# A decoder layer on one core: the sums of weight quarters in DRAM moved from the feed-forward part to the cross attention

## The chip, the cores and the metric

The kernel runs on one core of a Trainium2 chip. The core has five engines, each with its own queue that is worked through in order: TensorE (PE in the profile; loading of its stationary operand is shown apart as PEld), VectorE (DVE), ScalarE (ACT), GpSimd (POOL) and SyncE (SP). Transfers are issued from the queues of SP, ACT and POOL, and all of them run on the same 16 DMA engines of the core. An engine reaches an instruction only when those before it on its own queue are done, and waits there until the data that it names is ready.

The metric is the device time of one execution in microseconds; the median of the runs is compared.

## The reference

One decoder layer with 256 tokens and 256 memory tokens, D = 1024, all in float32:

```
z = x @ w_in                                     # pooling channels, q, k, v
mix = concat(pool(z_u), attention(z_q, z_k, z_v)) @ w_out
h1 = norm(alpha * x  + mix)
h2 = norm(alpha * h1 + cross_attention(h1, mem) @ w_xo)     # 4 heads of 256
h3 = norm(alpha * h2 + (silu(h2 @ w_gate) * (h2 @ w_up)) @ w_down)   # inner width 2816
```

The cross attention takes its queries from h1 @ w_xq, its keys and values from mem @ w_xkv.

## The kernel before

**Weights as two parts.** A product in float32 is made of three products of a faster type: each weight tile is rounded to a high part on ACT (line 171, `w49h`), and the remainder is a low part from DVE (line 173, `w49l`). The class `Stream` does this for all weights in one fixed order. A weight tile has a number: w43 to w50 are the query weights of the cross attention (two tiles for each of four heads), w51 to w58 its output projection, w59 to w102 gate and up, w103 to w123 six of the eleven chunks of the down projection in summed form, and so on.

**How the stream runs.** `fetch` issues the load of a tile on SP (line 103) into one of 7 raw buffers; a raw buffer comes free when its tile has been split. `prepare` gives a tile its high and low parts in one of 8 pairs of buffers, and then calls `fetch_ahead`. While a projection uses tile n, the tile 8 further on is cast. Where such a cast is called in the program, there it stands in the order of ACT and DVE, between their other work. `ws.before(n, load)` attaches another load to tile n: it is issued on SP just ahead of tile n's own load. The norm's gain and bias come in this way (ahead of w47 and w51 for the second norm).

**Stages.** Input projection and self attention; the mixing projection and first norm; the values of the memory tokens (`xv`) with the transposes of h1; then the queries of four heads (`do_xq`, `pxq`), with scores (`xscores`, `xs`), softmax, transposes and the products with the values between them; the output projection `xo`, during which the second norm's sums are made; the gate and up projections (`pg`) in eleven chunks; the down projection and third norm. The query of a head is drained from PSUM by ACT (line 849) and DVE (lines 850 and 852) before its scores can start (line 862). A norm needs one power of -0.5 of a column, which POOL computes (line 752).

**The sums in DRAM.** Seven of the eleven chunks of the down projection use a scheme with seven products in place of eight (Strassen's in Winograd's form). It needs sums of quarters of the weight. For six chunks these sums are made in DRAM, by DMAs that add to their target: `sum_z` and `sum_w` are DRAM buffers of 3 MB. Two plain copies, issued on SP, put two quarters in each, and four accumulating DMAs issued on POOL complete them. With the quarters numbered 0 to 3, sum_z becomes (1+2, 2+3), and sum_w becomes (0+1+2+3, 1+2+3). The sums are read as weight tiles from w105 on.

In the kernel before, the copy into sum_z is issued ahead of w62, the one into sum_w ahead of w63, and the four accumulations stand at the third chunk of gate and up (`add_quarters`). An accumulation waits for the copy or accumulation whose data it reads or adds to.

Of the kernel before, what the change touches and what calls it, by code (L numbers as in the profile page):

```python
# [11 lines left out]
OP = mybir.AluOpType  # L12
# [38 lines left out]
class Stream:  # L51
# [130 lines left out]
    def get(self, numbers, k):  # L182

        n = self.src[numbers[0]].shape[1]
        self.prepare(numbers[k // n] + 1)
        self.asked += 1
        if not self.held and self.asked % self.pace == 0:
            self.prepare(min(self.used + self.ahead, len(self.tiles) + 1))
        return self.parts_of(numbers, k)
# [18 lines left out]
def decoder_layer(  # L208
# [3 lines left out]
    nc = tc.nc  # L212
# [14 lines left out]
    def bank(name):  # L227
        return pb.tile([P, 512], F32, tag="b", name=name)

    def accbank(name):  # L230
        return pa.tile([P, 512], F32, tag="acc", name=name)


    ws = Stream(nc, rp, wp)

    def cols(w, c):

        return ws.add(w[c])

    def rows(w, k0, c0, nk=1, width=D):  # L240
        return ws.add(w[k0 * P:(k0 + nk) * P, c0:c0 + width].rearrange("(k p) n -> p k n", p=P), 1)
# [22 lines left out]
    c_xq = [cols(w_xq, c) for c in range(4)]  # L264
    c_xo = [rows(w_xo, k, 0) for k in range(KD)]
    c_gu = [ws.add(w_gu[c], 4) for c in range(NFC)]
    dram = ctx.enter_context(tc.tile_pool(name="dram", bufs=1, space=bass.MemoryType.DRAM))
    sum_z, sum_w = [dram.tile([P, 2, len(SUMMED), 512], F32, name=f"sum_{name}") for name in "zw"]
# [17 lines left out]
    class Both:  # L286
# [9 lines left out]
        def pair(self, k, ts=ALL):  # L296
            t, j = self.tiles[k // 4], k % 4
            return t[:, j, 0, ts], t[:, j, 1, ts]
# [51 lines left out]
    ws.before(c_dn[LAST[0]][1], load_norm("b", 3, ln3_b))  # L350


    ws.before(c_gu[0][3], lambda: nc.sync.dma_start(sum_z, w_sum[:, 1:3]))
    ws.before(c_gu[1][0], lambda: nc.sync.dma_start(sum_w, w_sum[:, 0:2]))

    def add_quarters():
        def add(dst, src):
            nc.gpsimd.dma_start(dst, src, accum_op=OP.add, max_dma_last_dim=8192)

        add(sum_z, w_sum[:, 2:4])  # L360
        for i in range(2):
            add(sum_w[:, i], sum_z[:, 1])
        add(sum_w[:, 0], w_sum[:, 1])

    ident = cp.tile([P, P], F32, name="ident")
    make_identity(nc, ident)
# [19 lines left out]
    def three(ps, w, y, start, stop, part=False):  # L386

        (wa, wb), (ya, yb) = w, y
        nc.tensor.matmul(ps, wa, ya, start=start, stop=False, skip_group_check=part)  # L389
        nc.tensor.matmul(ps, wa, yb, start=False, stop=False, skip_group_check=part)  # L390
        nc.tensor.matmul(ps, wb, ya, start=False, stop=stop, skip_group_check=part)  # L391
# [4 lines left out]
    def proj_both(pss, numbers, yT, group=KD):  # L396

        for k0 in range(0, KD, group):  # L400
            for k in range(k0, k0 + group):
                hi, _ = ws.get(numbers, k)
                for b, ps in enumerate(pss):
                    nc.tensor.matmul(ps, hi[:, b * P:(b + 1) * P], yT.both(k), start=k == 0, stop=False,  # L404
                                     skip_group_check=True)
                yield
            for k in range(k0, k0 + group):
                _, lo = ws.parts_of(numbers, k)
                for b, ps in enumerate(pss):
                    nc.tensor.matmul(ps[:, S:], lo[:, b * P:(b + 1) * P], yT.pair(k)[0], start=False,  # L410
                                     stop=k == KD - 1, skip_group_check=True)
                ws.done(numbers, k)
                if ws.pace == 1:
                    ws.next()
                yield

    def proj_n(pss, numbers, yT, last=True):

        for k in range(KD):
            for t, ps in pss.items():  # L420
                three(ps, yT.pair(k, slice(t * P, (t + 1) * P)), ws.get(numbers, k), k == 0, k == KD - 1)
            if last:
                ws.done(numbers, k)
            yield

    def proj_rows(acc, chunks, get, pieces, first, last, free, again=False):

        last_k = sum(ws.rows(numbers) for numbers in chunks) - 1
        k0 = 0
        for numbers in chunks:  # L430
            nk = ws.rows(numbers)
            for t in sorted({piece[0] for piece in pieces}):
                for j in range(nk):
                    k = k0 + j
                    y = pair(get(k), ALL, slice(t * P, (t + 1) * P))
                    hi, lo = ws.get(numbers, j)
                    for piece in pieces:
                        if piece[0] == t:
                            s = slice(*piece[1:])
                            three(acc[piece], y, (hi[:, s], lo[:, s]), first and k == 0, last and k == last_k,  # L440
                                  again)
                    if free and t == pieces[-1][0]:
                        ws.done(numbers, j)
                    yield
            k0 += nk

    def run(gen, n=None):

        while n is None or n > 0:
            if next(gen, gen) is gen:  # L450
                return False
            n = None if n is None else n - 1
        return True

    def split(h, l, ps):
        nc.scalar.copy(h, ps)  # L456
        nc.vector.tensor_sub(l, ps, r32(h))  # L457
# [267 lines left out]
    class Norm:  # L725
# [13 lines left out]
        def sum(self, c0, c1, acc):  # L739
            s = slice(c0, c1)  # L740
            nc.vector.scalar_tensor_tensor(self.r[:, s], self.tok[:, s], ALPHA, acc, op0=OP.mult, op1=OP.add)
# [39 lines left out]
    def project(chunks, get, held, pieces=PIECES):  # L781

        acc = {piece: accbank("acc") for piece in PIECES}
        if pieces != PIECES:
            (*_, (_, _, c), _), last = pieces, PIECES[-1]
            acc[pieces[-2]], acc[pieces[-1]] = acc[last][:, :c - last[1]], bank("acc")[:, :last[2] - c]
        head, rest = chunks[:-held], chunks[-held:]
        done = sum(ws.rows(numbers) for numbers in head)  # L790
        if head:
            yield from proj_rows(acc, head, get, PIECES, True, pieces != PIECES, True)
        ws.prepare(ws.used + ws.ahead)
        ws.prepare(ws.used + ws.ahead, nc.gpsimd)
        ws.held = True
        for piece in pieces:
            yield from proj_rows(acc, rest, lambda k: get(done + k), [piece], not head or piece[1] % 512 != 0, True,
                                 piece == pieces[-1], bool(head) and pieces != PIECES)
            yield piece, acc[last] if pieces != PIECES and piece == pieces[-2] else acc[piece]
# [77 lines left out]
    def xattend(h):  # L877
        po = bank("xo").rearrange("p (d t) -> p d t", d=2)
        for dd in range(2):
            for s in range(2):  # L880
                c = h * 256 + dd * P
                three(po[:, dd, :], pair(xv, ALL, s, slice(c, c + P)), pair(xpt[h], ALL, s), s == 0, s == 1)
        split(oT[0][:, 2 * h:2 * h + 2, :], oT[1][:, 2 * h:2 * h + 2, :], po)
# [18 lines left out]
    h2T = Both("h2T")  # L902
    h2 = ap.tile([P, T, D], F32, tag="a8", name="h2")
    xo = project(c_xo, lambda k: (oT[0][:, k], oT[1][:, k]), 4)
    xattend(1)
    run(xo, 1)
    xprobs_t(2)
# [56 lines left out]
    def gated_row(t, ps):  # L964

        sg = sg0[:, t, :]
        nc.scalar.activation(sg, ps[:, :CW], AF.Silu, bias=0.0, scale=1.0)
        nc.vector.tensor_mul(sg, sg, ps[:, CW:])
# [51 lines left out]
    ws.held = False  # L1020
    run(proj_n({1: first[1]}, c_gu[0], h2T))
    gated_row(1, first[1])
    left = None
    for c in range(1, NFC):
        pss = [(accbank if c % 2 else bank)("pg") for _ in range(4)]
        if c == 3:
            ws.widen(late)
            add_quarters()
        gu = proj_both(pss, c_gu[c], h2T, KD if c < NFC - 3 else 2)
        run(gu, 2)  # L1030
        if left:
            left.multiply()
        run(gu, 2)
        if left:
            left.split()
        else:
            run(gu, 4)
            gated_t()
        if c == NFC - 1:
            run(gu, 7)  # L1040
            ws.held = True
        run(gu)
        left = Gated(c, pss)
        left.add()
# [200 lines left out]
```

## Time and profile before

| | |
|---|---|
| median of 3 runs | 378.22 us (378.13 to 378.23) |
| the profiled execution | 378.57 us, its span 376.8 us |
| TensorE busy | 368.5 us, 98% of the span |
| DVE, ACT, POOL busy | 79%, 55%, 6% |
| granted TensorE clock, mean | 0.999 |
| moved by DMA | 90.80 MB, of it 7.86 MB by POOL's queue |

The profile is one execution. Its span runs from the first to the last instruction of the core, so it is a little shorter than the time of the execution. Its views are: busy time of each engine; the span in 40 equal slices of 9.4 us, with the busy share of each engine and of the DMA engines in tenths; the chain of work that ended last, followed back through what released each step; groups of instructions; what each engine waited for; timelines of single engines; and the DMA issues, with the time from issue to landing. In a row such as `w52h<-w52r 128x1024` the names are tiles of the program, `h`, `l` and `r` being the high part, the low part and the raw tile, and `SPq` is SP's queue issuing a DMA. In rows with two numbers in front, these are start and duration in us; what stands in square brackets is the idle time of the engine ahead of the row and what ended it.

### The profile page before, as it was taken

How to read it: one execution, taken by the hardware profiler on the slowest of the kernel's cores; microseconds unless marked ns; L12 is line 12 of the kernel's file. 1: busy time of each engine (PE TensorE's matmuls, PEld its weight loads, DVE VectorE, ACT ScalarE, POOL GpSimd, SP SyncE). 2: the span in 40 equal slices, each digit the busy share in tenths (PEclk: the TensorE clock that was granted, in tenths of full speed). 3: DMA queues.
4: the chain of work that ended last, by engine and by line, in shares of the span. 5: the costliest groups of instructions: out<-in, count | busy, mean ns of one | idle time of the engine just before them, and what ended most of it. 6: DMA issues, size and time to landing. Idle time of an engine off the chain costs nothing.

```text
span 376.8 us, 5614 instructions
## 1 busy us (share of the span) xinstructions
PE 368.5 (98%) x2058; PEld 317.2 (84%) x2058; DVE 298.2 (79%) x481; ACT 206.6 (55%) x330; POOL 24.5 (6%) x31
## 2 busy tenths in 40 slices
PE   9999999999999999999999999989999999999994
PEld 8997878787888889988888888868888888888882
DVE  6768799965699677865887468688888889989994
ACT  5746677644164636644145446465567668865510
POOL 1000033400010000000120101010000000000021
PEclk9999999999999999999999999999999999999999
DMA  7997674668509965998149999999655668996302
GB/s 268 414 416 270 217 286 139 198 221 285 165 0 301 374 214 181 348 334 315 57 79 232 340 272 355 291 318 335 236 192 172 199 195 255 300 401 260 94 0 111
DMA packets 26715, 90.80 MB, mean 241 GB/s; under 512 B 2624, under 2 KB 3392, under 8 KB 25920
## 3 DMA queue, kind: packets, MB, share of 16 engines
q1 hardware_dynamic: 25040, 82.13, 61.8%
q0 software_dynamic: 1216, 7.86, 10.3%
q10 hardware_dynamic: 432, 0.46, 0.3%
q8 instruction: 16, 0.26, 0.3%
q14 instruction: 11, 0.09, 0.1%
HBM read 89.39 MB, written 15.20 MB: 278 GB/s over the span
## 4 chain that ended last, share of the span: by engine, by line
PE 96%; DVE 1%; DMA 1%; ACT 1%; issue 0%; POOLq 0%; ACTq 0%
PE pg L404 20%; PE pg L410 10%; PE pqk L510 6%; PE m L389 5%; PE m L391 5%; PE m L390 5%; PE acc L389 4%; PE acc L390 4%; PE acc L391 4%; PE pxk L404 4%; PE pxq L404 4%; PE pxq L410 2%; PE pu L404 2%; PE pxk L410 2%; PE xv L389 2%; PE xv L391 2%
## 5 line engine op out<-in xcount | busy, mean ns | idle before, releaser
L456 ACT CAST g<-sg 128x512 fp32r<-128x512 f32 x16 | 9.9, 620 | 20.7 <-DVE sg L1010 14.8
L752 POOL TENSOR_TENSOR rs<-rs,mhalf 128x1 f32<-128x1 f32 x6 | 5.0, 832 | 238.5 <-DVE rs L751 238.5
L457 DVE TENSOR_TENSOR g<-sg,g 128x512 fp32r<-128x512 f32 x16 | 11.1, 692 | 9.6 <-ACT g L456 9.6
L991 DVE TENSOR_TENSOR sg<-pg,sg 128x256 f32<-128x256 f32 x40 | 14.1, 416 | 0.0
L990 ACT COPY sg<-pg 128x256 f32<-128x256 f32 x40 | 11.8, 378 | 0.6 <-PE pg L410 0.6
L995 ACT ACTIVATE sg<-sg 128x512 f32<-128x512 f32 x10 | 6.4, 635 | 10.0 <-DVE sg L991 10.0
L547 ACT ACTIVATE xpr<-xs,mx 128x256 f32<-128x256 f32 x8 | 3.7, 469 | 14.3 <-DVE mx L558 14.3
L547 ACT ACTIVATE pr<-pr,mx 128x128 f32<-128x128 f32 (+1 forms) x16 | 7.1, 445 | 7.6 <-DVE mx L578 7.6
L456 ACT CAST h2T<-tp 128x512 fp32r<-128x512 f32 x4 | 2.3, 586 | 13.0 <-PE tp L467 12.9
L757 DVE SCALAR_TENSOR_TENSOR r<-r,mv,gb 128x512 f32<-128x512 f32 (+2 forms) x12 | 8.2, 722 | 0.0
L744 DVE BATCH_NORM_STATS2 st<-r 128x6 f32<-128x512 f32 (+1 forms) x12 | 8.0, 670 | 0.3
L623 POOL TENSOR_TENSOR win<-upad 128x542 f32<-128x542 f32 x2 | 4.0, 1998 | 57.0 <-DVE upad L654 57.0
L996 DVE TENSOR_TENSOR sg<-sg 128x512 f32<-128x512 f32 x10 | 6.9, 691 | 0.8
L552 DVE RECIPROCAL sm<-sm 128x2 f32<-128x2 f32 x12 | 2.0, 166 | 6.0 <-ACT xpr L547 4.5
L862 PE MATMUL xs<-xkTh,xq 128*128 128x256 f32 x32 | 6.4, 282 | 0.0
L456 ACT CAST h1T<-tp 128x512 fp32r<-128x512 f32 x4 | 2.4, 588 | 7.1 <-PE tp L467 7.1
L762 DVE SCALAR_TENSOR_TENSOR h<-r,rs,gb 128x512 f32<-128x512 f32 x8 | 5.7, 747 | 0.1
L623 POOL TENSOR_TENSOR win<-win 128x269 f32<-128x269 f32 (+3 forms) x4 | 5.8, 1445 | 0.2
L662 ACT CAST xkTh<-pxk 128x256 fp32r<-128x256 f32 x8 | 2.6, 377 | 5.5 <-PE pxk L410 5.5
L664 DVE TENSOR_TENSOR xkl<-pxk,xkTh 128x256 f32<-128x256 f32 x8 | 3.0, 416 | 3.1 <-ACT xkTh L662 3.1
L862 PEld LDWEIGHTS xs<-xkTh,xq 128*128 128x128 f32 x32 | 5.2, 190 | 0.2
L171 ACT CAST w39h<-w39r 128x1024 fp32r<-128x1024 f32 x1 | 1.0, 1049 | 7.8 <-PE acc L391 7.8
(1132 smaller groups left out, 1286.4 us busy)
## 6 DMA issues: line engine op xcount, KB each, us to landing
sum_z<-in_w_sum SPq DMA_DIRECT2D x1, 3072.0 KB, 13.5
sum_w<-in_w_sum SPq DMA_DIRECT2D x1, 3072.0 KB, 18.8
sum_z<-in_w_sum POOLq DMA_DIRECT2D x1, 3072.0 KB, 21.1
sum_w<-sum_z POOLq DMA_DIRECT2D x2, 1536.0 KB, 15.6
gb<-in_ln_g SPq DMA_DIRECT2D x3, 512.0 KB, 6.2
gb<-in_ln_b SPq DMA_DIRECT2D x3, 512.0 KB, 9.2
sum_w<-in_w_sum POOLq DMA_DIRECT2D x1, 1536.0 KB, 14.6
wr<-in_w_qkv SPq DMA_DIRECT2D x5, 256.0 KB, 4.4
```

What stands on the lines that cost most here:

```text
L389: nc.tensor.matmul(ps, wa, ya, start=start, stop=False, skip_group_check=part)
L390: nc.tensor.matmul(ps, wa, yb, start=False, stop=False, skip_group_check=part)
L391: nc.tensor.matmul(ps, wb, ya, start=False, stop=stop, skip_group_check=part)
L404: nc.tensor.matmul(ps, hi[:, b * P:(b + 1) * P], yT.both(k), start=k == 0, stop=False, skip_group_check=True)
L410: nc.tensor.matmul(ps[:, S:], lo[:, b * P:(b + 1) * P], yT.pair(k)[0], start=False, stop=k == KD - 1, skip_group_check=True)
L456: nc.scalar.copy(h, ps)
L457: nc.vector.tensor_sub(l, ps, r32(h))
L510: nc.tensor.matmul(qk[i][:, f, :], w[:, c * P:(c + 1) * P], y, start=k == 0 and f == 0 and w is hi and y is x_hi, stop=k == KD - 1 and w i ...
L547: nc.scalar.activation(dst[:, j, :], src[:, j, :], AF.Exp, bias=mx[:, j:j + 1], scale=sign, accum_out=sm[:, j:j + 1])
L862: nc.tensor.matmul(ps[:, t, :], q[:, kk, t * P:(t + 1) * P], k[:, 2 * h + kk], start=n == 0, stop=q is q_lo and kk == 1, skip_group_check= ...
L990: nc.scalar.copy(y[:, f, :], ps[:, S:])
L991: nc.vector.tensor_add(y[:, f, :], ps[:, :S], y[:, f, :])
```

## The change

The same two copies and four accumulations are made, of the same bytes. Only their places differ:

- the copy into sum_z is issued ahead of w49 (the fourth head's query weights) instead of w62, and the copy into sum_w ahead of w52 (the second tile of the output projection) instead of w63;
- the accumulation into sum_z and the one into the second half of sum_w stand in front of the cross attention of the second head, where the output projection is set up, and so ahead of the second norm on POOL's queue;
- the two accumulations into the first half of sum_w stand behind the first gate chunk, and so behind the second norm on POOL's queue.

```diff
-    ws.before(c_gu[0][3], lambda: nc.sync.dma_start(sum_z, w_sum[:, 1:3]))
-    ws.before(c_gu[1][0], lambda: nc.sync.dma_start(sum_w, w_sum[:, 0:2]))
-
-    def add_quarters():
-        def add(dst, src):
-            nc.gpsimd.dma_start(dst, src, accum_op=OP.add, max_dma_last_dim=8192)
-
-        add(sum_z, w_sum[:, 2:4])
-        for i in range(2):
-            add(sum_w[:, i], sum_z[:, 1])
-        add(sum_w[:, 0], w_sum[:, 1])
+    ws.before(c_xq[3][0], lambda: nc.sync.dma_start(sum_z, w_sum[:, 1:3]))
+    ws.before(c_xo[1][0], lambda: nc.sync.dma_start(sum_w, w_sum[:, 0:2]))
+
+    def accumulate(dst, src):
+        nc.gpsimd.dma_start(dst, src, accum_op=OP.add, max_dma_last_dim=8192)
...
     xo = project(c_xo, lambda k: (oT[0][:, k], oT[1][:, k]), 4)
+    accumulate(sum_z, w_sum[:, 2:4])
+    accumulate(sum_w[:, 1], sum_z[:, 1])
     xattend(1)
...
     run(proj_n({1: first[1]}, c_gu[0], h2T))
     gated_row(1, first[1])
+    accumulate(sum_w[:, 0], sum_z[:, 1])
+    accumulate(sum_w[:, 0], w_sum[:, 1])
     left = None
     for c in range(1, NFC):
         pss = [(accbank if c % 2 else bank)("pg") for _ in range(4)]
         if c == 3:
             ws.widen(late)
-            add_quarters()
```

## The prediction

> **What bounds the kernel now.** I read the profile's page first, then what TensorE waits for, then the chain of work that ended last around the one wait, then the timelines of SP, ACT, DVE and POOL with the list of DMA issues. Times are microseconds from the span's start.
>
> ```profile
> PE 368.5 (98%) x2058; PEld 317.2 (84%) x2058; DVE 298.2 (79%) x481; ACT 206.6 (55%) x330; POOL 24.5 (6%) x31
> DMA  7997674668509965998149999999655668996302
> q1 hardware_dynamic: 25040, 82.13, 61.8%
> q0 software_dynamic: 1216, 7.86, 10.3%
> ```
> ```profile
> PE pg L404 <- DVE sg L991: 1.9, 1, 1.9
> ```
> ```profile
> 244.81 1.06 ACT w83h L171
> 245.89 1.23 DVE w83l L173
> ```
>
> TensorE is busy 98% of the span, and in the middle of the kernel it waits only once for more than 0.2 us: 1.9 us. The chain shows that wait: ACT rounds weight tile w83, DVE forms its low part, and only then does DVE (line 991) drain the PSUM banks that TensorE wants. The line of tenths says why the weight was late: the DMA engines are full in slices 21 to 27, counted from 0 (198 to 264 us), where the accumulating DMAs run beside the weights. So 1.9 us is the most that this change can win. Nobody waits for the sums themselves, as these rows of POOL and SP say:
>
> ```profile
> 244.78 1.15 POOL L358 DMA_DIRECT2D sum_w<-in_w_sum  x1 [14.79 <-issue]
> ```
> ```profile
> 288.83 0.62 SPq L103 DMA_DIRECT2D w105r<-sum_z  x1
> ```
>
> The last accumulation is issued at 244.8, and the first read of a sum at 288.8.
>
> **Where the copies go.** The two plain copies (3 MB each, DRAM to DRAM) stay on SP's queue. sum_z moves from in front of w62 to in front of w49, that is right behind w48; sum_w moves to right in front of w52. Rows of SP's timeline, and of the list of DMA issues (last number: us from issue to landing):
>
> ```profile
> 114.95 0.33 SPq L103 DMA_DIRECT2D w48r<-in_w_xq  x1
> ...
> 119.50 0.33 SPq L103 DMA_DIRECT2D w52r<-in_w_xo  x1
> ...
> 145.76 0.33 SPq L103 DMA_DIRECT2D w61r<-in_w_gu  x1
> 146.14 0.62 SPq L353 DMA_DIRECT2D sum_z<-in_w_sum  x1
> 152.16 0.33 SPq L103 DMA_DIRECT2D w62r<-in_w_gu  x1
> 152.54 0.52 SPq L354 DMA_DIRECT2D sum_w<-in_w_sum  x1
> 153.29 0.41 SPq L103 DMA_DIRECT2D w63r<-in_w_gu  x1
> ```
> ```profile
> sum_z<-in_w_sum SPq DMA_DIRECT2D x1, 3072.0 KB, 13.5
> sum_w<-in_w_sum SPq DMA_DIRECT2D x1, 3072.0 KB, 18.8
> ...
> w48r<-in_w_xq SPq DMA_DIRECT2D x1, 512.0 KB, 6.8
> ...
> w52r<-in_w_xo SPq DMA_DIRECT2D x1, 512.0 KB, 9.8
> ...
> w61r<-in_w_gu SPq DMA_DIRECT2D x1, 512.0 KB, 5.0
> w62r<-in_w_gu SPq DMA_DIRECT2D x1, 512.0 KB, 10.4
> w63r<-in_w_gu SPq DMA_DIRECT2D x1, 512.0 KB, 20.0
> ```
>
> Issue plus latency is the landing. w61 lands at 150.8, sum_z at 159.6, w62 at 162.6, sum_w at 171.3, w63 at 173.3: the order of issue. A weight behind a copy waits for the whole copy. The price of a copy: 159.6 - 150.8 = 8.8 us for the first. The second has w62 between itself and the first; q1 moved 82.13 MB in 61.8% of 376.8 us, 2.84 us per MB, so a weight of 0.52 MB is 1.5 us, and the second copy is 171.3 - 159.6 - 1.5 = 10.2 us. I take the mean, 9.5, and keep both as bounds.
>
> In the kernel before, these copies push w62 and w63, which nothing needs for long. At the new place the slack is small. w48 lands at 121.8 and w52 at 129.3. Rows of ACT, of DVE, and of the chain:
>
> ```profile
> 134.11 1.05 ACT L171 CAST w52h<-w52r 128x1024 fp32r<-128x1024 f32 x1 [0.76 <-PE pxq L404]
> 135.91 0.66 ACT L849 ACTIVATE xq<-pxq 128x256 fp32r<-128x256 f32 x2 [0.74 <-PE pxq L410]
> ```
> ```profile
> 136.27 1.22 DVE L173 TENSOR_TENSOR w52l<-w52r,w52h 128x1024 fp32r<-128x1024 f32 x1
> 137.40 0.42 DVE L850 SCALAR_TENSOR_TENSOR xql<-pxq,xq 128x256 f32<-128x256 f32 x1
> ```
> ```profile
> 139.19 1.43 PE xs L862 x12
> ```
>
> ACT casts w52 at 134.1, 4.8 us after its landing. Next in ACT's order is the evacuation of the first query head (xq), which DVE completes in four steps from 137.40 on, behind w52's low part; the last of them lets TensorE start the first scores at 139.19. So from a late w52 the delay runs straight into TensorE, although TensorE needs w52 itself only much later, in the output projection.
>
> **First term, the copies alone.** Both stand ahead of w52: it lands at 129.3 + 2 x 9.5 = 148.3. Everything else between w48 and w52 is there before as well. SP is not held: the copies wait for nothing, and each takes only 0.5 to 0.6 us to issue.
>
> **Second term, the accumulation that follows.** POOL's rows:
>
> ```profile
> 184.49 0.99 POOL L752 TENSOR_TENSOR rs<-rs,mhalf 128x1 f32<-128x1 f32 x1 [74.54 <-DVE rs L751]
> 190.97 0.55 POOL L752 TENSOR_TENSOR rs<-rs,mhalf 128x1 f32<-128x1 f32 x1 [5.50 <-DVE rs L751]
> 191.51 1.44 POOL L358 DMA_DIRECT2D sum_z<-in_w_sum  x1
> 212.96 1.16 POOL L358 DMA_DIRECT2D sum_w<-sum_z  x1 [20.01 <-DMA sum_z<-in_w_sum]
> ```
>
> POOL does not issue where the code stands but when its queue is free and the data is there: the add written at the third gate chunk goes out at 191.51, right behind the second norm's power. In the changed kernel POOL is free for the 74.5 us before 184.49, so the first accumulation goes out when sum_z has landed, at 121.8 + 9.5 = 131.3, while w49 to w52 and sum_w are still queued. Its bytes go through the same 16 engines. q0 needed 10.3% of 376.8 us, 38.8 us, for 7.86 MB; the 3.15 MB of this one are 15.5 us. By 133 it competes with about 15 us of q1's work up to w52 (148.3 - 133), so with half of the engines' time or more it is through when w52 lands: 148.3 + 15.5 = 163.8. Bounds: 0, if q1 goes first, and the 20.0 us that POOL waited for the landing (212.96's row). I take 15.5, since q0's row is of the same kind of work.
>
> By the Trainium skill, "DMA: Bandwidth & Descriptors", section "Anatomy of one DMA", a DMA from GpSimd takes about 2.0 us plus its bytes at 436 GB/s, which is 9.2 us for 3.15 MB. The same accumulation lasted 1.44 + 20.01 = 21.5 us here, and by the page's price w52 would land 6.3 us earlier, and the kernel would take 400.2 us.
>
> **From w52 to TensorE.** w52 at 163.8, its cast 1.05, its low part 1.22, DVE's four steps for xq with the start of the scores 139.19 - 137.40 = 1.79: the first scores start at 167.9 instead of 139.19, a stall of 28.7 us. w49 also comes late and blocks ACT, but earlier in the same queue, so it lies inside this. The weights behind w52 follow 1.5 us apart, and their casts stand in ACT's order behind the late evacuation and move with it: nothing more for them.
>
> **The clock.** The idle stretch also costs granted clock. Rows of TensorE's timeline at the start, of the chain, and of a table by stage:
>
> ```profile
> 0.78 3.17 PE L480 MATMUL busy<-const-float32-0.0 128*128 128x128 f32 x14 [0.78 <-PEq L1204]
> ```
> ```profile
> 62.32 0.43 PE pm L634 x2
> ```
> ```profile
> 372.00:376.80 4.80, 0.88 (x2) 0.27 (x2) 1.25 (x3) 0.48 (x1) 0.00 (x0) 0.89 0.30 109
> ```
>
> The opening 14 matmuls take 3.17/14 = 0.23 us for 128 columns of fp32; in mid-kernel the pooling matmul (256 columns, same type) takes 0.43/2 = 0.22, half per column. And in the last 4.8 us, when TensorE has almost stopped, the granted clock is 0.89. So after 28 us of idling I expect some 3 us at half speed: 1.5 us, between 0 and 3.
>
> **The later half.** The second accumulation (1.5 MB, 7.8 us by the same row) waits for the first and for sum_w: issue near 164, beside w53 and the weights after it, whose casts have moved by 28.7 us; a weight took 20.0 us at worst in the rows above, so I cost it at nothing. Without that cover it is up to its own 7.8 us. POOL is then free long before the power at 184.49 + 28.7. The two accumulations left behind the norm are 15.5 us of engine time where 38.8 stood, so the backlog that made w83 late is gone: -1.9 us; bounds 0 and -1.9.
>
> **Sum.** 28.7 + 1.5 - 1.9 = +28.3 us. The profiled execution took 378.57 us (span 376.8), which gives 406.9; the median of the runs is 378.22, and the forecast 406.5.
>
> **The rivals.**
> - *The copies cost, the accumulation does not.* If q1's packets go first, w52 lands at 148.3, the scores start at 152.4, the stall is 13.2: 378.2 + 13.2 + 1.5 - 1.9 = 391.0. For it: the accumulation needs its own start after 131.3. Against it: full engines whenever both queues have work (slices 21 to 27), with w83 late there. Chance, with cases between this and the forecast, 0.17.
> - *Hidden (faster).* The copies use engine time that is idle (slices 11, 14 and 19 are at 0, 6 and 1 tenths) and only the 1.9 us remain: 376.3. It would need w52 to land by 134.1, so both copies together to cost under 4.8 us, or weights to overtake them. w62 and w63, at 10.4 and 20.0 us, speak against it. Chance 0.06. The Trainium skill, the same page, "Rules for kernel authors", advises this: issue a DMA early, compute, wait on it late. Here the trace shows that a transfer issued early stands ahead of others with less slack.
> - *The power waits on POOL.* The second accumulation is queued ahead of the second norm's power, and waits for the first to land. It decides only if that comes after 184.49 + 28.7 = 213.2; a landing at 220 would give 413. The 49 us of margin leave it 0.03.
> - *Nothing measurable.* Gain and delay cancel within 0.2% (0.8 us, about what a measurement of this kernel can tell): 0.02.
>
> **How the numbers follow.** The forecast's own case has 0.72 and reaches from 400 (a cheaper accumulation) to 412.4: copies of 10.2 add 1.4, an accumulation of 20.0 adds 4.5, together 412.4. The range runs down to the first rival with copies of 8.8, 391.0 - 1.4 = 389.6, so 390.0 to 412.4, and leaves out the hidden case and the power. Faster 0.06, same 0.02, slower 0.92.
>
> **What would show it.** Right: in the changed profile sum_z and w52 land near 131 and 164; ACT idles for DMA on w49 to w52; TensorE waits some 28 us for the first xs; the granted clock falls there; the wait of 1.9 us on w83 is gone; POOL issues the first accumulation near 131. Wrong: w52 cast near 134, or at 148 with the accumulation landing far later, or the power of the second norm held by a DMA.

## The result and the profile after

The changed kernel takes 402.31 us (median of six, 399.35 to 403.42) against 378.18 us for the kernel before (377.83 to 378.60): a ratio of 1.0626, interval 1.0588 to 1.0664. The profiled execution took 402.81 us, its span is 401.0 us, 24.2 us longer than before.

The page of the changed kernel has TensorE busy for 93% of the span. There is a hole in slices 14 and 15 and part of 16 (counted from 0, 10 us each), and the granted clock falls there (`PEclk`); the DMA engines are full through the whole of it.

```profile
PE   8999999999999900799999999999999999999994
...
PEclk9999999999999965699999999999999999999999
DMA  7995856676159999995340999766665655698302
```

In the list of what TensorE waited for there is one new long wait, at the scores of the first head, for ACT's evacuation of its query; the other new ones are 0.3 us and less. The old wait for the banks of the gate products is not in the list any more.

```profile
PE xs L856 <- ACT xq L843: 22.2, 1, 22.2
```

Why ACT was late stands in its timeline (idle time ahead of a row, and what ended it, in brackets):

```profile
161.46 1.04 ACT L171 CAST w52h<-w52r 128x1024 fp32r<-128x1024 f32 x1 [21.18 <-DMA w52r<-in_w_xo]
162.41 0.65 ACT L843 ACTIVATE xq<-pxq 128x256 fp32r<-128x256 f32 x2
```

ACT stands 21.2 us in front of the cast of w52, and the query's evacuation comes right behind that cast. TensorE's rows for the first and the last of these scores:

```profile
162.84 0.58 PE L856 MATMUL xs<-xkTh,xq 128*128 128x256 f32 x1 [22.20 <-ACT xq L843]
...
165.40 1.01 PE L856 MATMUL xs<-xkTh,xq 128*128 128x256 f32 x3 [0.21 <-DVE xq L846]
```

The issues on SP, and the DMA issues with the time to landing:

```profile
115.88 0.88 SPq L353 DMA_DIRECT2D sum_z<-in_w_sum  x1
...
119.87 0.52 SPq L354 DMA_DIRECT2D sum_w<-in_w_sum  x1
121.19 0.34 SPq L103 DMA_DIRECT2D w52r<-in_w_xo  x1
```
```profile
sum_z<-in_w_sum SPq DMA_DIRECT2D x1, 3072.0 KB, 16.0
sum_w<-in_w_sum SPq DMA_DIRECT2D x1, 3072.0 KB, 33.8
sum_z<-in_w_sum POOLq DMA_DIRECT2D x1, 3072.0 KB, 32.3
...
w52r<-in_w_xo SPq DMA_DIRECT2D x1, 512.0 KB, 40.2
```

sum_z lands at 131.9, sum_w at 153.7, and w52, issued at 121.2, at 161.4. The accumulation is at work during nearly all of the second copy and all of w52. From 132.2 to 161.4 us the packets of SP's queue took 51.3% of the time of the 16 engines and those of POOL's queue 51.1%: the two queues shared the engines in halves. POOL's rows show when the accumulation went out, and that it was long through when the second norm's power came:

```profile
132.16 1.44 POOL L357 DMA_DIRECT2D sum_z<-in_w_sum  x1 [21.66 <-DMA sum_z<-in_w_sum]
164.77 1.16 POOL L357 DMA_DIRECT2D sum_w<-sum_z  x1 [31.18 <-DMA sum_z<-in_w_sum]
211.13 1.00 POOL L746 TENSOR_TENSOR rs<-rs,mhalf 128x1 f32<-128x1 f32 x1 [45.20 <-DVE rs L745]
```

**Where the 24.2 us come from.** The same instructions in TensorE's timeline, first of the kernel before, then of the changed one:

```profile
140.46 0.63 PE L404 MATMUL pxq<-h1T,w46h 128*128 128x512 f32 x2
...
142.83 1.55 PE L404 MATMUL pxq<-h1T,w47h 128*128 128x512 f32 x6
...
234.45 2.00 PE L404 MATMUL pg<-h2T,w75h 128*128 128x512 f32 x8
...
259.07 2.00 PE L404 MATMUL pg<-h2T,w83h 128*128 128x512 f32 x8
```
```profile
166.21 1.05 PE L398 MATMUL pxq<-h1T,w46h 128*128 128x512 f32 x2
...
169.46 1.55 PE L398 MATMUL pxq<-h1T,w47h 128*128 128x512 f32 x6
...
261.09 2.00 PE L398 MATMUL pg<-h2T,w75h 128*128 128x512 f32 x8
...
283.31 2.00 PE L398 MATMUL pg<-h2T,w83h 128*128 128x512 f32 x8
```

Right behind the first scores (the rest of w46) the changed kernel is 166.21 - 140.46 = 25.75 us late. At w47 it is 26.63 us late: another 0.88 us, from the half clock. At w75 it is still 26.64 us late, and at w83 24.24: the stretch in which the kernel before waited 1.9 us is 2.4 us shorter. Of the 25.75 us, 0.55 was there from the opening (the load of w46 is issued at 113.23 instead of 112.68), where the change does nothing. So 25.2 + 0.9 - 2.4 + 0.55 = 24.2.

### The profile page after: what moved, and what is told of

Same layout as the page of the kernel before. It is cut to its first block, busy times and chain, and to the rows that moved or that the text cites. A ratio compares the mean times of both kernels' runs of the same rounds, so it can differ in the third digit from the quotient of the medians.

```text
span 401.0 us, 5615 instructions
## 1 busy us (share of the span) xinstructions
PE 371.5 (93%) x2058; PEld 319.4 (80%) x2058; DVE 297.9 (74%) x481; ACT 206.6 (52%) x330; POOL 24.5 (6%) x31
## 4 chain that ended last, share of the span: by engine, by line
PE 57%; DMA 12%; DVE 3%; ACT 0%; issue 0%; POOLq 0%; DVEq 0%; ACTq 0%; SPq 0%
PE pg L398 18%; DMA w52r<-in_w_xo 10%; PE pg L404 10%; PE m L384 4%; PE m L383 4%; PE m L385 4%; PE pxq L398 2%; PE acc L383 2%; PE acc L384 2%; PE acc L385 2%; DMA w47r<-in_w_xq 2%; PE pxq L404 2%; PE xs L856 1%; PE pg L385 1%; PE pg L383 1%; PE pg L384 1%
## 5 line engine op out<-in xcount | busy, mean ns | idle before, releaser
L856 PE MATMUL xs<-xkTh,xq 128*128 128x256 f32 x32 | 8.1, 327 | 22.4 <-ACT xq L843 22.2
L856 PEld LDWEIGHTS xs<-xkTh,xq 128*128 128x128 f32 x32 | 6.2, 222 | 23.3 <-ACT xq L843 22.6
L173 DVE TENSOR_TENSOR w52l<-w52r,w52h 128x1024 fp32r<-128x1024 f32 x1 | 1.2, 1226 | 21.0 <-ACT w52h L171 21.0
L171 ACT CAST w52h<-w52r 128x1024 fp32r<-128x1024 f32 x1 | 1.0, 1044 | 21.2 <-DMA w52r<-in_w_xo 21.2
L991 ACT ACTIVATE sg<-sg 128x512 f32<-128x512 f32 x10 | 6.4, 636 | 10.5 <-DVE sg L987 10.5
## 6 DMA issues: line engine op xcount, KB each, us to landing
sum_z<-in_w_sum POOLq DMA_DIRECT2D x1, 3072.0 KB, 32.3
```

What stands on the lines that cost most here:

```text
L856: nc.tensor.matmul(ps[:, t, :], q[:, kk, t * P:(t + 1) * P], k[:, 2 * h + kk], start=n == 0, stop=q is q_lo and kk == 1, skip_group_check= ...
```

## The experiments

Each ratio is to the kernel before, measured beside the run: 377.90 us for experiments 1, 2, 3 and 7, 378.24 us for 4, 5 and 6. The diffs of 1, 2, 3, 5 and 7 are against the changed kernel, those of 4 and 6 against the kernel before; line numbers differ by a few between the kernels.

**1. The copies alone.** The copies stay at their new places; all accumulations go back to the third gate chunk.

```diff
-    accumulate(sum_z, w_sum[:, 2:4])              # at the output projection
-    accumulate(sum_w[:, 1], sum_z[:, 1])
...
-    accumulate(sum_w[:, 0], sum_z[:, 1])          # behind the first gate chunk
-    accumulate(sum_w[:, 0], w_sum[:, 1])
...
         if c == 3:
             ws.widen(late)
+            accumulate(sum_z, w_sum[:, 2:4])
+            for i in range(2):
+                accumulate(sum_w[:, i], sum_z[:, 1])
+            accumulate(sum_w[:, 0], w_sum[:, 1])
```

> Both copies at their new places (ahead of w49 and w52), all four accumulations at their old place. Theory (each piece of work that the DMA engines do ahead of w52 holds ACT, and through it TensorE's first scores): w52 lands near 149 instead of 129.3, TensorE waits some 11 us for the first xs, the accumulations run as before and the old wait of 1.9 us stays: 378.2 + 11.4 + 0.9 (clock) = 390.5 us, about half of the loss. Rival A (the accumulation is the cause, plain copies fit in): under 381. Rival B (the accumulation costs nothing there): 402, as the changed kernel.

Measured: 391.09 us, ratio 1.0344 (1.0322 to 1.0366). ACT's timeline and TensorE's waits:

```profile
148.33 1.04 ACT L171 CAST w52h<-w52r 128x1024 fp32r<-128x1024 f32 x1 [10.23 <-DMA w52r<-in_w_xo]
```
```profile
PE xs L856 <- ACT xq L843: 10.4, 1, 10.4
PE pg L398 <- DVE sg L985: 1.3, 1, 1.3
```

w52 is cast at 148.3, as it lands: 19.0 us later than it landed before (129.3), twice the 9.5 us put down for a copy. In the changed kernel it is cast 13.1 us later still (161.46). Of this 0.7 us lies in the opening (w46 is issued at 113.23 there, at 112.51 here), so the accumulation holds w52 for 12.4 us. The wait in the gate products is back, at 1.3 us, with the accumulations behind the norm; so the kernels' times are 11.2 us apart. Both parts of the change carry the loss, and neither carries it alone.

**2. The accumulations alone.** The copies go back to w62 and w63; the accumulations stay at their new places.

```diff
-    ws.before(c_xq[3][0], lambda: nc.sync.dma_start(sum_z, w_sum[:, 1:3]))
-    ws.before(c_xo[1][0], lambda: nc.sync.dma_start(sum_w, w_sum[:, 0:2]))
+    ws.before(c_gu[0][3], lambda: nc.sync.dma_start(sum_z, w_sum[:, 1:3]))
+    ws.before(c_gu[1][0], lambda: nc.sync.dma_start(sum_w, w_sum[:, 0:2]))
```

> Both copies at their old places (ahead of w62 and w63), the accumulations at their new places in the program, so two of them ahead of the second norm on POOL's queue. Theory: w49 to w52 are in time, no wait at the first xs. The first accumulation goes out when sum_z lands, near 160, and shares the engines with the copy of sum_w and with w63 and w64, so it lands near 188; the second waits for it on POOL, and the power due at 184.5 stands behind it: TensorE waits some 5 us at the transposes of h2; the later wait of 1.9 us is gone: 381.5 us, between 377 and 384. Rival (POOL's order costs nothing): 376.3, no wait at the transposes.

Measured: 383.60 us, ratio 1.0145 (1.0123 to 1.0167). POOL's timeline, TensorE's wait, and stages around it:

```profile
189.41 1.16 POOL L357 DMA_DIRECT2D sum_w<-sum_z  x1 [27.87 <-DMA sum_z<-in_w_sum]
190.16 1.02 POOL L746 TENSOR_TENSOR rs<-rs,mhalf 128x1 f32<-128x1 f32 x1
```
```profile
PE tp L461 <- DVE h L756: 4.4, 1, 4.4
```
```profile
186.00:192.00 6.00, 1.64 (x8) 1.02 (x6) 0.88 (x3) 0.00 (x0) 1.76 (x2) 0.85 1.00 372
192.00:197.00 5.00, 4.98 (x16) 4.20 (x17) 4.86 (x10) 1.17 (x2) 0.55 (x1) 0.50 1.08 279
```

The rival of the prediction that had 49 us of margin in the changed kernel becomes real here: the second accumulation stands on POOL until the first has landed, at 189, and the power behind it, ready from 184.8 on, starts at 190.2. TensorE waits 4.4 us at the transposes of h2. The time was expected at 381.5 us; what was left out is the clock. In the last column but two of the second stage it is 0.50: after a wait of only 4.4 us TensorE ran 5 us at half speed, which costs about 2.5 us more. So the accumulations at the new place are not harmless: with the copies early they add 11.2 us to the time, with the copies late they hold the norm.

**3. The casts held back.** The changed kernel, with one difference: no weight is cast ahead of its use while the four query projections run. (`held` is a switch that `Stream` has already: while it is set, a tile is cast only when it is used.)

```diff
+    ws.held = True
     run(xq[0])
...
     run(xq[3])
+    ws.held = False
```

> The changed kernel, with the casting of weights ahead of their use held back during the four heads' query projections, and let go again at the output projection: w50 and later tiles are cast when first used. Theory (TensorE waits because the cast of w52 stands in ACT's order in front of the query's evacuation, not because it needs w52): w52 still lands near 161, but the first scores start within 2 us of their old time; a smaller wait, 2 to 6 us, comes at the output projection, where w51 and w52 are cast on demand: 380 to 386 us. Rival (what TensorE lacks is the late weights themselves, or DMA time in general): 398 to 403.

Measured: 383.53 us, ratio 1.0140 (1.0115 to 1.0165). w52 takes 37.6 us from its issue at 121.6, so it lands at 159.2, almost as late as in the changed kernel. But ACT's evacuation, and TensorE's waits, are these:

```profile
136.81 0.69 ACT L843 ACTIVATE xq<-pxq 128x256 fp32r<-128x256 f32 x2
```
```profile
PE acc L383 <- ACT w51h L171: 1.6, 1, 1.6
...
PE pxq L398 <- ACT w50h L171: 1.2, 1, 1.2
...
PE acc L384 <- DVE w51l L173: 0.8, 1, 0.8
```

The query is evacuated at 136.8 instead of 162.4, and 18.8 us of the loss are gone, with the same DMAs in the same order (from w57 on the loads go out later, since raw buffers come free later). So TensorE did not lack the weight: it lacked ACT, which stood in front of a cast whose product is needed some 30 us later.

**4. The holding by itself.** The kernel before, with the same two lines.

> The kernel before, with the same holding back of casts as in the run with the changed kernel: what the holding costs by itself. Theory (the 5.6 us left over in that run are the on-demand casts of w50 and w51, and no late load): 381 to 384 us, with waits of TensorE for the casts of w50 and w51. Rival (the rest in that run was late loads): 378 to 379.

Measured: 389.16 us, ratio 1.0281 (1.0260 to 1.0302): the expectation was wrong. TensorE's waits and a stage:

```profile
PE tp L467 <- DVE h L762: 3.3, 1, 3.3
...
PE acc L389 <- ACT w51h L171: 1.6, 1, 1.6
...
PE pxq L404 <- ACT w50h L171: 1.2, 1, 1.2
...
PE acc L390 <- DVE w51l L173: 0.8, 1, 0.8
```
```profile
142.00:165.00 23.00, 19.69 (x131) 17.34 (x129) 13.51 (x29) 9.60 (x24) 0.00 (x0) 1.00 0.07 24
```

The three waits for on-demand casts are the same as in experiment 3 (1.6, 1.2, 0.8), so there they belong to the holding and not to late loads. What the expectation missed: raw buffers that are not cast are not refilled, so the DMA engines stand at 0.07 of their time from 142 to 165, and the copies, tied to w62 and w63, go out 25 us later (171.5 instead of 146.1), into the transfers for the gate products. w62 then holds ACT for 3.6 us, TensorE waits 3.3 us at the transposes, and the clock is at half for 3.4 us behind that. The old wait in the gate products is there too (1.7 us). These numbers are of the profiled execution (387.84 us). With the 3.6 us of the three casts, less the 1.9 us of the old wait before, they account for all but about 1 us of the 9.3 by which its span is longer. With casts held, the places of the changed kernel are the better ones (383.5 against 389.2).

**5. One copy early.** Only the copy into sum_z is at its new place; the rest is as before.

```diff
-    ws.before(c_xo[1][0], lambda: nc.sync.dma_start(sum_w, w_sum[:, 0:2]))
+    ws.before(c_gu[1][0], lambda: nc.sync.dma_start(sum_w, w_sum[:, 0:2]))
```
(with the accumulations as in experiment 1)

> Only the copy into sum_z at its new place (ahead of w49); the copy into sum_w and all four accumulations at their old places. Theory (what lies ahead of w52 is paid for only beyond the slack of some 5 us that w52 has on ACT, and about 3 us that TensorE has from that cast to the first scores): one copy of 9.5 us makes w52 land near 139, and TensorE waits 1 to 2.5 us for the first xs: 379.5 to 381 us. Rival (the loss goes with the bytes moved, half of them for half the loss): 378.2 + 6 = 384.

Measured: 380.90 us, ratio 1.0070 (1.0051 to 1.0090).

```profile
138.32 1.05 ACT L171 CAST w52h<-w52r 128x1024 fp32r<-128x1024 f32 x1 [0.24 <-DMA w52r<-in_w_xo]
```
```profile
PE pg L398 <- DVE sg L985: 1.3, 1, 1.3
PE xs L856 <- DVE xq L846: 1.3, 2, 0.9
```

One copy costs 2.7 us, two cost 13.2 (391.09 against 377.90 beside it). The first 9.5 us of work ahead of w52 are mostly covered by the slack; what comes on top is paid in full (the second copy moves the cast of w52 by 10.0 us and the time by 10.5). The loss does not go with the bytes.

**6. Four and five tiles later.** The kernel before, with the copies ahead of w53 and w57.

```diff
-    ws.before(c_gu[0][3], lambda: nc.sync.dma_start(sum_z, w_sum[:, 1:3]))
-    ws.before(c_gu[1][0], lambda: nc.sync.dma_start(sum_w, w_sum[:, 0:2]))
+    ws.before(c_xo[2][0], lambda: nc.sync.dma_start(sum_z, w_sum[:, 1:3]))
+    ws.before(c_xo[6][0], lambda: nc.sync.dma_start(sum_w, w_sum[:, 0:2]))
```

> Both copies still in the cross attention, but four and five tiles later: the copy into sum_z ahead of w53, the one into sum_w ahead of w57; all four accumulations at their old place. Theory: w49 to w52 are in time; w53 lands near 141 (cast at 142), w57 near 157 (cast near 158), so no wait, and the old wait of 1.9 us stays: 378 us, between 377.5 and 379.5. Rival (3 MB copies during the cross attention cost TensorE or the engines something by themselves, as in the run with the copies alone): 385 to 391.

Measured: 378.10 us, ratio 0.9999 (0.9986 to 1.0013). The DMA issues and ACT's casts:

```profile
w53r<-in_w_xo SPq DMA_DIRECT2D x1, 512.0 KB, 18.2
...
w57r<-in_w_xo SPq DMA_DIRECT2D x1, 512.0 KB, 19.8
```
```profile
142.69 1.04 ACT L171 CAST w53h<-w53r 128x1024 fp32r<-128x1024 f32 x1
...
158.17 1.06 ACT L171 CAST w57h<-w57r 128x1024 fp32r<-128x1024 f32 x1
```

w53 is issued at 121.6 and lands at 139.8, 2.9 us ahead of its cast; w57 is issued at 134.5 and lands at 154.3, 3.9 us ahead. Neither row has idle time in front. The same 6 MB, issued 5 and 12 us later than in experiment 1 (120.3 and 131.3 instead of 115.2 and 119.2), cost nothing when they stand behind the tiles whose casts precede the first query, instead of in front of them. (This moves the copies without the accumulations; experiment 1 is its counterpart.)

**7. A faster split.** The copies at their old places; ahead of the norm on POOL only the one accumulation that nobody on POOL waits behind, and the three others behind the first gate chunk.

```diff
     xo = project(c_xo, lambda k: (oT[0][:, k], oT[1][:, k]), 4)
     accumulate(sum_z, w_sum[:, 2:4])
-    accumulate(sum_w[:, 1], sum_z[:, 1])
...
-    accumulate(sum_w[:, 0], sum_z[:, 1])
+    for i in range(2):
+        accumulate(sum_w[:, i], sum_z[:, 1])
     accumulate(sum_w[:, 0], w_sum[:, 1])
```
(with the copies as in experiment 2)

> Copies at their old places; the accumulation into sum_z alone ahead of the second norm on POOL's queue, the three half-size ones behind the first gate chunk. Theory: sum_z's accumulation goes out near 160 and lands near 188, no one waits for it on POOL ahead of the powers, w63 (cast at 196) is still in time, and 23 us of accumulation are left behind the norm instead of 38.8, so that w83 is no longer late: 376.3 us, 0.5% faster than before. Rival (some 16 us of accumulation beside the copy of sum_w and w63 to w67 make w63 late, or the rest is still enough to hold w83): 378.2 or more.

Measured: 376.40 us, ratio 0.9958 (0.9943 to 0.9973): 0.4% faster than the kernel before, a small gain but clear of the interval. All that TensorE still waits for:

```profile
PE end L1182 <- ACT diag L1179: 1.5, 1, 1.5
PE busy L474 <- PEq L1201: 0.8, 1, 0.8
PE pqk L504 <- ACT w0h L171: 0.4, 1, 0.4
PE acc L383 <- DVE xkTl L660: 0.2, 1, 0.2
```
```profile
161.22 1.44 POOL L357 DMA_DIRECT2D sum_z<-in_w_sum  x1 [51.16 <-DMA sum_z<-in_w_sum]
184.61 0.99 POOL L746 TENSOR_TENSOR rs<-rs,mhalf 128x1 f32<-128x1 f32 x1 [21.96 <-DVE rs L745]
```

Only its start, the end and two waits under half a microsecond are left. The first accumulation runs from 161 to 190, in part over engine time that the kernel before left idle (its DMA engines are busy 78% of the time from 170 to 180 us and 17% from 180 to 190), and the power is on time at 184.6. Of the 1.9 us that the prediction named as the most to be won, this gets 1.5 (376.40 against 377.90 beside it).

## Why the prediction was right

The forecast was 406.5 us, the measured time is 402.31 us: +24.1 us where +28.3 was forecast. The chain of causes was right. The time alone would not show that, since the stated range also takes in the first rival, where the copies alone cost; POOL's row at 132.16, the halves in which the two queues shared the engines, and experiment 1 decide between them. By its steps:

- *Where it stalls*: right. w52's cast, then the query's evacuation, then the first scores, with cast and evacuation in that order on ACT; experiment 3 shows that this order is the cause, experiments 5 and 6 that the slack of w52 decides.
- *First term, the copies, 9.5 us each*: right. Experiment 1 has w52 19.0 us late.
- *Second term, the accumulation, 15.5 us*: too large, it was 12.4. It was taken to be through when w52 lands; it landed at 164.5, 3.1 us after w52. By the formula of the Trainium skill ("DMA: Bandwidth & Descriptors", section "Anatomy of one DMA") an estimate of 9.2 us would have stood here; the measurement lies half way between 9.2 and 15.5. The whole accumulation took 32.3 us beside the copy, and 20.7 us beside a few weights (experiment 1).
- *From w52 to TensorE*: the chain was sized right, but not all scores wait for it. From w52's landing to the start of the last three products (165.40) it is 4.0 us, where 4.06 was put down. But eight of the twelve products of the scores use only the high part of the query, which ACT alone makes (the description of the kernel, too, lets them wait for DVE): TensorE began at 162.8 and did these, at half clock, while DVE finished. The row at 139.19 was misread for the same reason: in the kernel before TensorE came to the scores straight from w46 and waited for nobody, and that DVE was done at about the same time (139.06) is a coincidence. By the time scale of the kernel before, w52 landed 2.9 us earlier than forecast, and the early start of the scores saved another 0.6, which makes 25.2 us of the 28.7.
- *The clock, 1.5 us*: the fall is there, 0.9 us of it behind the scores; the rest lay beside the wait for DVE.
- *The later half, -1.9 us*: right in kind, -2.4 measured, since the wait had also slowed the products behind it (those of w79 took 2.34 us in the kernel before, and 2.00 in the changed one). No power waited, as the margin said.
- *The power waiting on POOL*: rightly small in this kernel. It was priced without the clock; experiment 2 shows the mechanism at 4.4 us of waiting and 2.5 us lost to half speed.
- *The rival with the copies alone*, 391.0, comes out at what experiment 1 measured (391.09), in part by luck: it has the old wait gone (-1.9), which experiment 1 shortens by only 0.6 us, and against that a clock term of 1.5 where experiment 1 lost 0.5. It is not this kernel, because the accumulation does take its turn.
- *Hidden*: false for this place. Four and five tiles later the copies do hide (experiment 6), though with the accumulations at their old place nothing is won by it. The advice of the Trainium skill ("DMA: Bandwidth & Descriptors", section "Rules for kernel authors") to issue early does no harm there, and costs 24 us where what is issued stands in front of a load with less slack.

## What to carry to other kernels

A transfer that nobody waits for still has a place in a queue: look at what is issued behind it, how much slack that has, and on which engine its consumer stands in order. A load that is late by more than its slack stops everything behind its first use on that engine, whether or not the bound engine needs that load. And a DMA issue that waits for data blocks the small work queued behind it on its engine: put it there only if its data comes before that work is due, as the faster split does.

## What the runs showed of the hardware

**Short waits can cost clock.** The changed kernel's long wait takes the granted clock to half, and it stays there for some microseconds after TensorE starts again (the last column but two is the clock):

```profile
142.00:165.00 23.00, 2.16 (x9) 2.05 (x9) 2.39 (x5) 1.60 (x3) 0.23 (x1) 0.55 1.01 264
165.00:167.00 2.00, 1.79 (x6) 1.47 (x6) 0.90 (x2) 0.00 (x0) 0.93 (x1) 0.50 1.04 426
167.00:169.00 2.00, 2.00 (x14) 1.93 (x13) 0.88 (x4) 1.82 (x5) 0.00 (x0) 0.71 1.03 420
```

That was expected. Not expected was that 4.4 us of waiting were enough (experiment 2), with 5 us of half speed behind them, so that the wait cost about one and a half times its length. The single wait of 1.9 us in the kernel before left the clock at full: there the stage from 240 to 252 us has 1.00. But the length of a wait alone does not decide: in experiment 3 the waits of 1.6 and 0.8 us, with 0.5 us of work between them, brought 3.4 us of half clock, and the same two waits in experiment 4 brought none.

The stretches at half clock last 23.9 us in the changed kernel, 10.2 in experiment 1, 6.8 in experiment 2, and 3.4 in experiments 3 and 4 (there behind the wait of 3.3 us). These are 7, 3, 2, 1 and 1 times 3.41 us. The fall came between 2.5 us (experiment 2) and 4.6 us (experiment 1) after TensorE's last product, and the return 5.3 us after the restart in the changed kernel, 4.4 in experiment 1 and 5.0 in experiment 2. This fits a clock that is set anew every 3.41 us, whenever the wait begins; what TensorE must do in such a step to keep it is not shown. The Trainium skill ("TensorE: Matmul & The Clock Gate", Part 1) gives one window of about 3.4 us or more of idling for the fall, and of work for the return. The step length and the returns agree with it; the fall after 2.5 us came sooner.

**A copy in DRAM is a long block in its queue.** 3 MB from DRAM to DRAM held the weights behind them for 9 to 10 us in each of the places tried (8.8 and 10.2 in the kernel before, 19.0 for two in experiment 1, 8.9 in experiment 5, 9.2 for w53 in experiment 6), beside 1.3 us for a weight of 0.5 MB in a full queue (w53 and w54 of the kernel before land at 130.6 and 131.9).
